# GpSimd's weight splits in the input and up projections of a two-layer encoder trunk, done by accumulating transfers from the fourth pair on

## Chip, cores and metric

One Trainium2 chip, one core. The metric is the time of one execution of the program on the device in microseconds (us): the median of three runs of the kernel before, 2488.0 us (2484.28 to 2490.77). In the text PE is TensorE, ACT is ScalarE, DVE is VectorE, POOL is GpSimd and SP is SyncE.

## What is computed

The program runs two layers on a sequence of 1024 positions with 1024 features, all in float32. Per layer:

```
h = rmsnorm(x, norm1_w)
q, k, v, g, z, xbc, dt, lru_gate, lru_x = split(h @ w_in)       # input projection
y = concat(retention(q, k, v, g), ssd(z, xbc, dt), rglru(lru_gate, lru_x))
x = x + y @ w_out
h = rmsnorm(x, norm2_w)
u, v = split(causal_conv3(h @ w_up))                            # up projection, 2 x 2816 columns
x = x + (gelu(u) * v) @ w_down
```

A last RMSNorm follows the second layer. The change touches the weights of the two products `h @ w_in` and `h @ w_up`.

## The kernel before

**Precision.** Every matrix operand is kept as two tiles of the fp32r type: the high part `hi`, a rounded copy, and the low part `lo = raw - hi`. A product is three passes over the pair: hi with hi, hi with the low part of the activations, and the low part of the weights with hi. PE therefore reads the low part of a weight tile in the third pass, behind two passes that need the high part alone.

**Splitting a weight.** `part_split` (L232) makes the two parts of a 128 x 512 piece: ACT writes the high part (L233), then DVE or POOL subtracts (L234). `lo_engine` hands the subtraction out in turn: in the input and up projections every third one goes to DVE, the other two to POOL (`share[0] = 3`). The two parts are the halves of one tile named `ws`; there are eight such tiles.

**Pairs.** The columns of both projections are worked off in pairs of 128-column tiles (class `Pair`), 12 pairs for `w_in` and 22 for `w_up` in each layer. A pair is computed with a Strassen-like scheme: seven products of twelve 128 x 512 matmuls each. Two raw tiles `wr` of 128 x 1024 (three buffers) are loaded per pair; the first holds blocks a11 and a12, the second a21 and a22. `start` splits a11 and a12 and makes two products. `prep` then works on the raw tiles in place: DVE subtracts a21 from a11 and a second tile `s2` is made from a22 and that; POOL adds a22 to a21 and subtracts `s2` from a12 (all L706); each of the five results is split. `end` makes five products, and DVE and ACT fetch all of them from PSUM. What comes out goes through a causal convolution (`conv`: ACT L311, then DVE L314, one instruction per tap), an activation, and to DRAM.

**Order.** `products` walks the pairs. The first three of each projection have another form (`lead`, `start(True)`), so that PE has work while the norm of the second half of the sequence is being computed; from `j = 3` on a pair is `start` and `end`. The order of the instructions on each engine is decided when the program is built, by a scheduler that goes by its own estimates of durations; each engine then runs its list in order and waits on semaphores.

**Stages** of the profiled execution, by its times: the fourth and later pairs of the input projection run from 113 to 343 us and from 1332 to 1548 us, those of the up projection from 627 to 995 us and from 1836 to 2205 us. Between them lie the mixers with the output projection, and the down projection.

Of the kernel before, what the change touches and what calls it, by code (L numbers as in the profile page):

```python
# [8 lines left out]
F32 = mybir.dt.float32  # L9
F32R = mybir.dt.float32r  # L10
I32 = mybir.dt.int32
AF = mybir.ActivationFunctionType
ALU = mybir.AluOpType
# [37 lines left out]
def hybrid_trunk(  # L51
# [13 lines left out]
    act, dve, pool, pe, sp = nc.scalar, nc.vector, nc.gpsimd, nc.tensor, nc.sync  # L65
# [131 lines left out]
    def lo_engine():  # L197
        flip[0] += 1
        return dve if flip[0] % share[0] == 0 else pool
# [20 lines left out]
    def wsplit(src, n=KD * P):  # L220

        raw = wr.tile([P, 2 * HT], F32, tag="wr", name=nm("wr"))
        last_dma[0] = sp.dma_start(raw[:, :n], src)
        out_ = []
        m = n // 2
        for o in (0, m):
            w = w_tile()
            part_split(w, raw[:, o : o + m], m)
            out_.append(w)
        return out_  # L230

    def part_split(w, raw, m, eng=None):  # L232
        act.activation(w[:, 0, :m], raw, AF.Copy)  # L233
        (eng or lo_engine()).tensor_tensor(w[:, 1, :m], raw, w[:, 0, :m].bitcast(F32), op=ALU.subtract)  # L234

    def wk(w):
        return lambda k, a: w[k // 4][:, a, P * (k % 4) : P * (k % 4) + P]
# [534 lines left out]
    def part_of(src):  # L772
        w = w_tile()
        part_split(w, src, HT)
        return w
# [117 lines left out]
    def products(pairs, rest, later, lead, ahead, raw=False):  # L893

        n = lead + ahead
        for j, p in enumerate(pairs[:n]):
            if j < lead:
                p.lead(raw)
            else:
                p.start(True, raw)  # L900
            if j < n - 1:
                rest(j)
        rest(2)
        for j, p in enumerate(pairs):
            if j >= n:
                p.start()
            elif raw:
                p.scaled()
            if j == 1:
                rest(3)  # L910
            if j < lead:
                p.follow()
            else:
                p.end()
            for f in later.get(j, ()):
                f()

    def ffn_pair(l, j, B):
        u = {}

        def take(m, h, x, then=None):
            cw = fcw[:, l, 2 * j + m, :]
            t = t_tile("fc")
            conv(t, x, lambda i: cw[:, i : i + 1], cw[:, 3:4], 3, not h, then)
            if m == 0:
                u[h] = t
                act.activation(t, t, AF.Gelu_apprx_tanh)  # L927
                return
            dve.tensor_mul(t, u[h], t)
            sp.dma_start(gscr[l][j][:, h, :], t)  # L930

        return Pair((w_up[l, 2 * j], w_up[l, 2 * j + 1]), B, take)
# [30 lines left out]
    def ffn_down(l, after):  # L963
# [95 lines left out]
        def last(lo=0, hi=HT, hook=None):  # L1059

            e = slice(lo, hi)
            for i in range(NP):
                w = W[i]
                t = w_tile()
                part_split(t[:, :, e], G[i][1][:, e], hi - lo, pool)
                for oc in range(4):
                    for k, (x, y) in enumerate(PASSES):
                        pe.matmul(X[oc][:, e], w[x][:, P * oc : P * oc + P], t[:, y, e], start=False, stop=i == NP - 1 and k == 2, skip_group_check=True)
                if hook:
                    hook(i)  # L1070
            for o in range(4):
                dve.tensor_add(u[o][:, e], u[o][:, e], X[o][:, e])
# [338 lines left out]
```

## Time and profile before

| | |
|---|---|
| three runs, median | 2488.0 us |
| lowest, highest | 2484.28, 2490.77 us |
| the profiled execution, own time | 2486.72 us |
| its span, first to last instruction | 2484.9 us |
| PE busy | 2236.0 us, 90% of the span |
| DVE busy | 2120.7 us, 85% |
| POOL busy | 1258.0 us, 51% |
| ACT busy | 1125.4 us, 45% |
| busy share of the 16 DMA engines (queue 1, issued by SP) | 36.3% |
| mean granted clock of PE | 0.956 |

The shares are means over stages with different limits, so the prediction reads each stage by itself: busy time by stretch, groups of instructions by line in a stretch, and who waited for whom. A duration given for one instruction is that of a row. The granted clock is a fraction of PE's full speed.

### The profile page before, as it was taken

Reading aid. Unit: us, or ns where it says so; the run is one execution under the profiler, and the core shown is the slowest. Engines: PE = TensorE matmul, PEld = TensorE weight load, DVE = VectorE, ACT = ScalarE, POOL = GpSimd, SP = SyncE. Lnnn points to the kernel's source line nnn. Section 1 sums busy time; section 2 is a strip of 40 time slices with the busy share of each in tenths; the row PEclk is TensorE's granted clock in tenths of the full one; section 3 lists DMA queues with packets and bytes.
Section 4 is the critical chain, followed back from the end, with each engine's and each line's share of the span. In section 5 each row is a group of like instructions: output and inputs, shape, how many; then the busy total and the mean of one; then the engine's idle time right before and its main releaser. Section 6 shows DMA issues by size and latency. Waiting matters only on the chain. (4 is left out here: it accounts for less than half of the span.)

```text
span 2484.9 us, 31513 instructions
## 1 busy us (share of the span) xinstructions
PE 2236.0 (90%) x10646; PEld 1774.6 (71%) x10646; DVE 2120.7 (85%) x3242; ACT 1125.4 (45%) x2110; POOL 1258.0 (51%) x846
## 2 busy tenths in 40 slices
PE   6788888997999999889988889789889999988997
PEld 4566667775888887667765768677668888866776
DVE  7998879668999999987789977785799999999787
ACT  4335437454344444434443463664534444443343
POOL 4545543346555455554655444334475555547443
PEclk8989989999999999999989989899999999999999
DMA  4321267551222222844333214846322222255521
GB/s 172 98 82 65 81 222 231 157 195 43 94 85 77 85 77 85 272 155 127 102 111 102 85 51 142 284 127 197 128 72 77 77 86 84 77 191 179 170 75 69
DMA packets 138706, 303.76 MB, mean 122 GB/s; under 512 B 15280, under 2 KB 27696, under 8 KB 138544
## 3 DMA queue, kind: packets, MB, share of 16 engines
q1 hardware_dynamic: 135760, 297.55, 36.3%
q10 hardware_dynamic: 2784, 4.20, 0.5%
q8 instruction: 84, 1.38, 0.2%
q14 instruction: 78, 0.64, 0.1%
HBM read 228.22 MB, written 69.27 MB: 120 GB/s over the span
## 5 line engine op out<-in xcount | busy, mean ns | idle before, releaser
L296 PE MATMUL up<-bh,ws 128*128 128x512 f32 x3840 | 1228.0, 399 | 46.0 <-ACT bh L202 17.3
L296 PEld LDWEIGHTS up<-bh,ws 128*128 128x128 f32 x3840 | 735.1, 192 | 224.4 <-ACT bh L202 25.3
L234 POOL TENSOR_TENSOR ws<-wr,ws 128x512 fp32r<-128x512 f32 x386 | 573.1, 1496 | 461.6 <-ACT ws L233 453.0
L296 PE MATMUL up<-bl,ws 128*128 128x512 f32 x1920 | 763.5, 399 | 40.7 <-DVE bl L203 20.5
L233 ACT ACTIVATE ws<-wr 128x512 fp32r<-128x512 f32 x568 | 340.0, 621 | 307.0 <-issue 73.3
L296 PEld LDWEIGHTS up<-bl,ws 128*128 128x128 f32 x1920 | 368.8, 192 | 137.3 <-DVE bl L203 29.6
L991 PE MATMUL dy<-ws,ws 128*128 128x512 f32 x792 | 219.3, 417 | 38.2 <-DVE ws L234 16.0
L314 DVE SCALAR_TENSOR_TENSOR fc<-u,smalls,fc 128x512 f32<-128x512 f32 (+2 forms) x176 | 215.1, 1225 | 25.7 <-ACT fc L311 24.4
L706 POOL TENSOR_TENSOR wr<-wr 128x512 f32<-128x512 f32 x64 | 114.1, 1783 | 216.7 <-DVE wr L706 192.6
L991 PEld LDWEIGHTS dy<-ws,ws 128*128 128x128 f32 x792 | 149.7, 196 | 97.4 <-DVE ws L234 36.1
L314 DVE SCALAR_TENSOR_TENSOR fc<-c,smalls,fc 128x512 f32<-128x512 f32 (+2 forms) x176 | 211.7, 1203 | 7.4 <-ACT fc L311 7.2
L991 PE MATMUL dx<-ws,ws 128*128 128x512 f32 x792 | 196.3, 398 | 1.5 <-DVE u L888 1.4
L234 DVE TENSOR_TENSOR ws<-wr,ws 128x512 fp32r<-128x512 f32 x182 | 160.0, 879 | 28.1 <-ACT ws L233 25.0
L991 PEld LDWEIGHTS dx<-ws,ws 128*128 128x128 f32 x792 | 152.7, 193 | 35.0 <-DVE u L888 1.8
L311 ACT ACTIVATE fc<-c,smalls 128x512 f32<-128x512 f32 x88 | 71.2, 810 | 214.3 <-DVE c L835 211.9
L296 PE MATMUL op<-yh,ws 128*128 128x512 f32 x512 | 162.4, 395 | 2.9 <-ACT yh L210 2.9
L706 POOL TENSOR_TENSOR wr<-wr,s 128x512 f32<-128x512 f32 x64 | 92.9, 1452 | 118.6 <-DVE u L316 97.3
L927 ACT ACTIVATE fc<-fc 128x512 f32<-128x512 f32 x88 | 55.7, 633 | 169.2 <-DVE fc L314 169.0
L234 DVE TENSOR_TENSOR ws<-g,ws 128x512 fp32r<-128x512 f32 (+1 forms) x94 | 113.9, 1238 | 20.8 <-ACT ws L233 20.6
L296 PEld LDWEIGHTS op<-yh,ws 128*128 128x128 f32 x512 | 95.5, 188 | 24.1 <-ACT yh L210 4.6
L234 POOL TENSOR_TENSOR ws<-g,ws 128x512 fp32r<-128x512 f32 (+1 forms) x71 | 103.4, 1466 | 3.8 <-ACT ws L233 3.0
L296 PE MATMUL op<-yl,ws 128*128 128x512 f32 x256 | 100.9, 397 | 1.3 <-DVE yl L215 0.8
(316 smaller groups left out, 3413.0 us busy)
## 6 DMA issues: line engine op xcount, KB each, us to landing
wr<-in_w_up_dram SPq DMA_DIRECT2D x96, 512.0 KB, 3.8
wr<-in_w_dn_dram SPq DMA_DIRECT2D x66, 512.0 KB, 3.6
wr<-in_w_ct_dram SPq DMA_DIRECT2D x56, 512.0 KB, 3.7
wr<-in_w_o_dram SPq DMA_DIRECT2D x32, 512.0 KB, 4.9
g0scr<-fc SPq DMA_DIRECT2D x44, 256.0 KB, 2.1
g<-g0scr SPq DMA_DIRECT2D x44, 256.0 KB, 5.6
g1scr<-fc SPq DMA_DIRECT2D x44, 256.0 KB, 2.1
g<-g1scr SPq DMA_DIRECT2D x44, 256.0 KB, 5.5
```

The costliest lines, as they stand in the source:

```text
L233: act.activation(w[:, 0, :m], raw, AF.Copy)
L234: (eng or lo_engine()).tensor_tensor(w[:, 1, :m], raw, w[:, 0, :m].bitcast(F32), op=ALU.subtract)
L296: pe.matmul(dst, W(k, a), A(k, b), start=first and i == 0, stop=last and i == n - 1)
L311: act.activation(dst, body(x), AF.Identity, bias=bias, scale=taps(n))
L314: dve.scalar_tensor_tensor(dst[:, o:HT], x[:, HALO - j + o : HALO - j + HT], taps(n - j), dst[:, o:HT], op0=ALU.mult, op1=ALU.add)
L706: eng.tensor_tensor(o, a, b, op=op)
L927: act.activation(t, t, AF.Gelu_apprx_tanh)
L991: pe.matmul(d[oc], w[:, a, P * oc : P * oc + P], t[:, b], start=not more and i == 0 and k == 0, stop=i == NP - 1 and k == 2, skip_group_ch ...
```

## The change

From the fourth pair of each projection on, a split that falls to POOL is no longer a subtraction on POOL. ACT writes the high part as before, then a second ACT instruction writes the negated high part into the low half, and a transfer issued from POOL's queue adds the raw weights onto it, from SBUF to SBUF. Splits that fall to DVE, and all splits of the first three pairs, of the output and the down projection, stay as they are.

```diff
+    by_dma = [False]
+
     def part_split(w, raw, m, eng=None):
         act.activation(w[:, 0, :m], raw, AF.Copy)
-        (eng or lo_engine()).tensor_tensor(w[:, 1, :m], raw, w[:, 0, :m].bitcast(F32), op=ALU.subtract)
+        eng = eng or lo_engine()
+        if eng is pool and by_dma[0]:
+
+            act.activation(w[:, 1, :m], w[:, 0, :m].bitcast(F32), AF.Copy, scale=-1.0)
+            pool.dma_start(w[:, 1, :m].bitcast(F32), raw, accum_op=ALU.add)
+            return
+        eng.tensor_tensor(w[:, 1, :m], raw, w[:, 0, :m].bitcast(F32), op=ALU.subtract)
...
         for j, p in enumerate(pairs):
+            by_dma[0] = j >= n
             if j >= n:
                 p.start()
...
             for f in later.get(j, ()):
                 f()
+        by_dma[0] = False
```

In the built program POOL's list has 851 rows before and after. 260 of its subtractions have become transfers (`DMA`, L240), and ACT's list has 261 more `ACTIVATE` rows. Lines behind L234 move by 8 to 10. The scheduler has also placed other instructions anew; two places matter for what follows.

POOL, one pair of the up projection in the first layer. `wr1260` is the pair's first raw tile (a11 and a12), `wr1268` its second; `ws1261` and `ws1262` are the splits of a11 and a12, the later `ws` those of the five combinations; `s21269` is `s2`. In brackets stands whose semaphores a row waits for (DMAHW: a transfer issued by SP or ACT, DMASW: one issued by POOL). Before:

```order
261 L234 TENSOR_TENSOR ws1261_6702<-wr1260_6700,ws1261_6702 128x512 [waits DMAHW1_49,Activation_49]
262 L706 TENSOR_TENSOR wr1268_6744<-wr1268_6744 128x512 [waits DMAHW4_49,DVE_49]
263 L234 TENSOR_TENSOR ws1262_6705<-wr1260_6700,ws1262_6705 128x512 [waits PE_49,Activation_49]
264 L706 TENSOR_TENSOR wr1260_6700<-wr1260_6700,s21269_6747 128x512 [waits DVE_49,Pool_49]
265 L234 TENSOR_TENSOR ws1271_6752<-wr1260_6700,ws1271_6752 128x512 [waits Activation_49]
266 L234 TENSOR_TENSOR ws1272_6756<-wr1268_6744,ws1272_6756 128x512 [waits Activation_49]
267 L234 TENSOR_TENSOR ws1274_6763<-wr1268_6744,ws1274_6763 128x512 [waits Activation_49]
```

The same rows in the changed program:

```order
261 L240 DMA ws1261_6776<-wr1260_6774 128x512 [waits DMASW5_49,DMASW2_49,DMAHW1_49,PE_49,Activation_49]
262 L240 DMA ws1262_6780<-wr1260_6774 128x512 [waits PE_49,Activation_49]
263 L714 TENSOR_TENSOR wr1268_6820<-wr1268_6820 128x512 [waits DMAHW4_49,DMASW1_49,DVE_49]
264 L714 TENSOR_TENSOR wr1260_6774<-wr1260_6774,s21269_6823 128x512 [waits DMASW3_49,DVE_49]
265 L240 DMA ws1271_6828<-wr1260_6774 128x512 [waits DMASW7_49,PE_49,Activation_49]
266 L240 DMA ws1272_6833<-wr1268_6820 128x512 [waits PE_49,Activation_49,Pool_49]
267 L240 DMA ws1274_6841<-wr1268_6820 128x512 [waits PE_49,Activation_49]
```

Five of the seven rows have become transfers, and the subtraction from a12 (row 264) now waits for the landing of the transfer in row 262, which reads a12.

DVE, at the same pair: its two subtractions on the raw tiles, and around them the convolution of the pair before (`fc`), the products of the up projection with `gelu` (L929) and the fetching of products from PSUM (`u`, `c` from `up`). Before:

```order
1070 L888 TENSOR_TENSOR u31227_6479<-u31227_6479,up1232_6516 128x512 [waits PE_49]
1071 L316 COPY c221228_6480<-u31227_6479 128x2 [waits DVE_49]
1072 L706 TENSOR_TENSOR wr1260_6700<-wr1260_6700,wr1268_6744 128x512 [waits DMAHW4_49,DMAHW1_49,Pool_49]
1073 L706 TENSOR_TENSOR s21269_6747<-wr1268_6744,wr1260_6700 128x512 [waits DVE_49]
1074 L314 SCALAR_TENSOR_TENSOR fc1233_6530<-u31227_6479,smalls_123,fc1233_6530 128x511 [waits Activation_49]
1075 L314 SCALAR_TENSOR_TENSOR fc1234_6537<-c221228_6480,smalls_123,fc1234_6537 128x512 [waits DMAHW2_49,Activation_49]
1076 L314 SCALAR_TENSOR_TENSOR fc1233_6530<-u31227_6479,smalls_123,fc1233_6530 128x510 [waits DVE_49]
```

In the changed program:

```order
1070 L896 TENSOR_TENSOR u31227_6549<-u31227_6549,up1232_6586 128x512 [waits PE_49]
1071 L324 COPY c221228_6550<-u31227_6549 128x2 [waits DVE_49]
1072 L322 SCALAR_TENSOR_TENSOR fc1233_6600<-u31227_6549,smalls_123,fc1233_6600 128x511 [waits Activation_49]
1073 L322 SCALAR_TENSOR_TENSOR fc1234_6607<-c221228_6550,smalls_123,fc1234_6607 128x512 [waits DMAHW2_49,DVE_49,Activation_49]
1074 L322 SCALAR_TENSOR_TENSOR fc1233_6600<-u31227_6549,smalls_123,fc1233_6600 128x510 [waits DVE_49]
1075 L322 SCALAR_TENSOR_TENSOR fc1234_6607<-c221228_6550,smalls_123,fc1234_6607 128x512 [waits DVE_49]
1076 L939 TENSOR_TENSOR fc1233_6600<-fc1217_6490,fc1233_6600 128x512 [waits DVE_49]
1077 L939 TENSOR_TENSOR fc1234_6607<-fc1231_6581,fc1234_6607 128x512 [waits DVE_49]
1078 L843 TENSOR_TENSOR c111241_6650<-u1240_6636,up1239_6623 128x512 [waits DMAHW3_49,PE_49,Activation_49]
1079 L714 TENSOR_TENSOR wr1260_6774<-wr1260_6774,wr1268_6820 128x512 [waits DMAHW1_49,DMAHW4_49,DMASW5_49,DMASW2_49]
```

The subtraction on `wr1260` has moved behind four taps, two products and the fetch of `up1239`, and it waits for the landing of the transfer that splits a11.

## Rows read from the trace of the kernel before

**Rows 1.** The page's first part: busy time, share of the span, instructions.
```profile
PE 2236.0 (90%) x10646; PEld 1774.6 (71%) x10646; DVE 2120.7 (85%) x3242; ACT 1125.4 (45%) x2110; POOL 1258.0 (51%) x846
```

**Rows 2.** Busy time by stretch: us, PE, PEld, DVE, ACT, POOL, granted clock, DMA share, GB/s.
```profile
113.00:343.00 230.00, 193.98 (x798) 150.49 (x796) 195.21 (x281) 100.79 (x165) 118.40 (x77) 0.93 0.27 89
...
627.00:995.00 368.00, 364.99 (x1600) 298.97 (x1599) 346.14 (x438) 157.90 (x260) 189.99 (x127) 1.00 0.24 84
...
1332.00:1548.00 216.00, 195.28 (x804) 151.77 (x803) 180.16 (x263) 101.10 (x166) 100.07 (x68) 0.93 0.26 87
...
1836.00:2205.00 369.00, 366.17 (x1603) 299.79 (x1602) 346.95 (x439) 158.17 (x260) 190.72 (x128) 1.00 0.24 84
```

**Rows 3.** The same of line L234 alone (the subtraction): us, DVE, POOL, clock, DMA.
```profile
113.00:343.00 230.00, 22.76 (x22) 63.48 (x43) 0.93 0.27 89
627.00:995.00 368.00, 39.21 (x45) 130.41 (x89) 1.00 0.24 84
```

**Rows 4.** In order of time, up projection: start us, us, engine, line, operation, out<-in.
```profile
740.50 0.33 SPq L779 DMA_DIRECT2D wr<-in_w_up_dram  x1
...
745.96 1.74 POOL L234 TENSOR_TENSOR ws<-wr,ws 128x512 fp32r<-128x512 f32 x1
...
746.48 1.77 DVE L314 SCALAR_TENSOR_TENSOR fc<-u,smalls,fc 128x510 f32<-128x510 f32 x1
...
748.18 0.74 DVE L314 SCALAR_TENSOR_TENSOR fc<-c,smalls,fc 128x512 f32<-128x512 f32 x1
```

**Rows 5.** Groups by line, DVE, 627 to 995 us: count | busy us, mean ns.
```profile
L314 DVE SCALAR_TENSOR_TENSOR fc<-c,smalls,fc 128x512 f32<-128x512 f32 (+1 forms) x74 | 93.3, 1261 | 3.5 <-ACT fc L311 3.5
L314 DVE SCALAR_TENSOR_TENSOR fc<-u,smalls,fc 128x510 f32<-128x510 f32 (+2 forms) x75 | 92.3, 1233 | 11.3 <-ACT fc L311 10.6
```

**Rows 6.** Groups by line, DVE, 113 to 343 us.
```profile
L314 DVE SCALAR_TENSOR_TENSOR xb<-c,smalls,xb 128x512 f32<-128x512 f32 (+3 forms) x23 | 21.5, 935 | 0.0
...
L314 DVE SCALAR_TENSOR_TENSOR xc<-u,smalls,xc 128x511 f32<-128x511 f32 (+2 forms) x6 | 6.4, 1075 | 0.0
```

**Rows 7.** Who PE waited for, 113 to 343 us: us in total, times, longest.
```profile
PE lgp L349 <- DVE xc L314: 15.5, 3, 8.5
PE cum L502 <- DVE da L499: 6.6, 1, 6.6
PE dtt L414 <- DVE dtc L409: 5.0, 1, 5.0
```

**Rows 8.** The same, 1332 to 1548 us.
```profile
PE lgp L349 <- DVE xc L314: 7.9, 2, 5.5
...
PE dtt L414 <- DVE dtc L411: 4.1, 1, 4.1
```

**Rows 9.** The same, 343 to 400 us.
```profile
PE up L296 <- DVE u L872: 6.1, 1, 6.1
```

**Rows 10.** The same, 995 to 1060 us.
```profile
PE dy L991 <- DVE u L877: 4.3, 1, 4.3
```

**Rows 11.** The same, 2205 to 2265 us.
```profile
PE dy L991 <- DVE u L877: 4.6, 1, 4.6
```

**Rows 12.** The same, whole span.
```profile
PE up L296 <- POOL ws L234: 2.0, 2, 1.6
```

**Rows 13.** DMA issues, 627 to 995 us: count, KB each, median us from issue to landing.
```profile
wr<-in_w_up_dram SPq DMA_DIRECT2D x36, 512.0 KB, 4.0
g0scr<-fc SPq DMA_DIRECT2D x38, 256.0 KB, 2.1
...
a<-in_w_dn_dram SPq DMA_DIRECT2D x2, 256.0 KB, 3.4
```

**Rows 14.** The page's part on DMA issues, whole span.
```profile
g<-g0scr SPq DMA_DIRECT2D x44, 256.0 KB, 5.6
```

**Rows 15.** The page's costliest groups, whole span.
```profile
L234 POOL TENSOR_TENSOR ws<-wr,ws 128x512 fp32r<-128x512 f32 x386 | 573.1, 1496 | 461.6 <-ACT ws L233 453.0
...
L233 ACT ACTIVATE ws<-wr 128x512 fp32r<-128x512 f32 x568 | 340.0, 621 | 307.0 <-issue 73.3
```

## The prediction

> **What bounds the kernel now.** I read the busy shares first [rows 1]. PE has 90%, DVE 85%, POOL 51%, ACT 45%: two engines lie close together, and which of them decides must be read by stretch. The table by stretch [rows 2] gives the four stretches in which splits change. In the two of the up projection PE is busy for 364.99 of 368 us and 366.17 of 369 at a granted clock of 1.00. There PE is the bound, and at most 3.0 + 2.8 = 5.8 us can be won. In the two of the input projection it is busy for 193.98 of 230 us and 195.28 of 216, at a clock of 0.93, so 36.0 + 20.7 = 56.7 us of PE time lie open. The list of waits says for whom: most of what it names is DVE, 15.5 + 6.6 + 5.0 = 27.1 us in the first input stretch [rows 7] and 7.9 + 4.1 = 12.0 in the second [rows 8]. Right behind the stretches PE waits again for DVE to empty PSUM: 6.1, 4.3 and 4.6 us [rows 9 to 11]. For a split by POOL it waits 2.0 us in the whole run [rows 12]. So in the input stretches, and where the stretches end, DVE's lateness costs PE time. POOL's splits are early enough.
>
> Then the rows in order of time [rows 4]. A tap on DVE takes 1.77 us while a split runs on POOL (745.96 to 747.70 us), and 0.74 us when none does. POOL's work thus makes DVE's instructions longer, and that is the way by which this change can win.
>
> **The change, part by part.**
>
> *260 subtractions leave POOL.* One costs 1.50 us [rows 15]. POOL waits for others half the time, so its own freed time is worth nothing; what counts is DVE's. In the up projection the taps take 74 x (1.261 - 0.74) + 75 x (1.233 - 0.74) = 38.6 + 37.0 = 75.6 us more than undisturbed [rows 4, 5]. The splits are 130.4 of POOL's 190.0 us there [rows 2, 3], 69%, so some 52 us of DVE's 346 go in 19 pairs, 2.7 us a pair. In an input stretch the bounds lie further apart. From above: 75.6/190.0 = 0.40 us of DVE for one us of POOL, times 63.5 us of splits [rows 3], 25 us. From below, two groups of taps alone: 23 x (0.935 - 0.74) + 6 x (1.075 - 0.74) = 6.5 us [rows 6], of which the splits' share (63.5 of 118.4) is 3.5 us. I take 15 us, nearer to the upper end since rows 6 are two groups out of many, and 14 for the second stretch: 29 us.
>
> How much of that does PE see? None if other waits take over, at most all 29. DVE is busy for 85 and 83% of these stretches and PE for 84 and 90%, so either bounds a part; I take three fifths, **-17 us**. In the up projection I take half of the 5.8, **-3 us**. At the ends of the stretches DVE will be less far behind; of 6.1 + 4.3 + 4.6 = 15.0 us I take two thirds, **-10 us**.
>
> *261 ACT instructions are added,* 0.62 us each [rows 15], 160 us over the four stretches, in which ACT is busy for 43 to 47% of the time [rows 2]. They lie beside PE's work and cost nothing as long as ACT is not late. Without that cover each would cost its 0.62 us, and one of them stands in the chain of every split.
>
> *260 transfers of 256 KB are added.* No row shows a transfer issued by POOL. Its issue I bound by SP's 0.33 us [rows 4] and by the 1.50 us of the instruction it replaces [rows 15], and take 1.0, between them. Its landing I bound by a plain store of this size, 2.1 us [rows 13], and by twice the landing of a load in the busiest stretch, 2 x 5.6 = 11.2 us [rows 14], because the accumulation reads two operands. I take 3.4, the load of this size into SBUF in the same stretch [rows 13], since the DMA engines are busy only 24 to 27% there [rows 2]. A split then ends later by 0.62 + 1.0 + 3.4 - 1.50 = 3.5 us; even with the lowest ends it ends later, by 1.6 us, so nothing is won by the transfer itself. For the price of a DMA from GpSimd, the Trainium skill, page "DMA: Bandwidth & Descriptors", section "Anatomy of one DMA — SWDGE (gpsimd) path", gives a fit of 2.0 us plus the bytes over 436 GB/s, by which 256 KB would take an estimated 2.6 us in all and the delay would be 1.7 us; no run here shows it.
>
> Where does the delay show? PE now waits twice for a split by POOL [rows 12]; both waits grow by 3.5: **+7 us**. All other splits have something in hand, and they start earlier where DVE, whose subtractions on the raw tiles stand ahead of them, is less late.
>
> *New waits.* The order of the changed program lets DVE's subtraction from a11 wait for the landing of a11's own split, and POOL's subtraction from a12 for the landing of a12's. Behind the first stand DVE's taps and all its fetches from PSUM, for which PE waits; behind the second POOL's further issues. In the up projection eight DVE instructions stand between the fetch of the last product and that subtraction, about 8 x 0.74 = 5.9 us. Meanwhile the split of a11 needs the fetch (0.74), three ACT instructions (3 x 0.62) and then issue and landing: 2.6 us plus 4.4. That is 1.1 us late, and DVE, with (346 - 52)/19 = 15.5 us of work in the 19.4 us of a pair, has 3.9 us to spare. So issue and landing together may take 3.3 + 3.9 = **7.2 us** before PE notices. The ring of raw tiles says much the same: load 4.0 [rows 13], two subtractions on DVE 1.5, one on POOL 1.5, seven ACT instructions 4.3, issue and landing 4.4 make 15.7 of 19.4 us, which bears 8.1 us of issue and landing. I therefore cost these waits at nothing, covered by PE's 19.4 us a pair.
>
> **Sum.** -17 - 3 - 10 + 7 = -23 us on the profiled execution's 2486.7 gives 2463.7. The median of the runs shown is 1.3 us above that execution, so I forecast **2465 us**.
>
> **The rivals.**
>
> *The relief does not reach the end.* If POOL holds DVE up while it makes a transfer, for the 1.0 us that I take instead of 1.50, only a third of the relief is left: -6 - 1 - 3 + 7 = -3, some 2485 us. Or the other waits of the input stretches (on ACT, on the clock) take over. For it: PE is as busy as DVE there. Against it: 39 us of waits name DVE. Chance 0.18; range 2478 to 2497.
>
> *Landings come late.* Place: DVE's subtraction from a11, in the two pairs of three whose a11 falls to POOL, 25 of the 38 pairs of the up projection. Price: 25 us for every us of issue and landing beyond 7.2. At 9 us that is +45; with two thirds of the gain kept, -16, 2487 + 29 = some 2515 us. At the upper ends, 1.5 + 11.2 = 12.7 us, it would be over 130 us. For it: DVE is busy for 94% of these stretches [rows 2], and a split on POOL takes up to 1.74 us where DVE works beside it [rows 4]; a transfer's issue from POOL could be held up likewise, and by more than one DVE instruction. Against it: the transfers of this stretch land in 2.1 to 4.0 us [rows 13]. The Trainium skill speaks for it on its page "SBUF — State Buffer", section "SBUF: two separate sides": a DMA issued from GpSimd starves while VectorE runs an instruction in a two-port performance mode, because GpSimd cannot write the descriptors then. In this kernel's stretches the DVE groups of rows 5 and 6 are two-input instructions, of which the same page, section "Who interferes with whom", says only by inference that they leave descriptor writing alone; the stretched 1.74 us agree with the shared port and do not settle that. Chance 0.22.
>
> *My forecast* has 0.60, with a range of its own from 2438 to 2479: below, three quarters of all that is open (39.1 + 5.8 + 15.0 = 59.9, so -45 and no late splits, 2443 with the median's 1.3, and a little for the granted clock of 0.93); above, two thirds of the gain lost.
>
> **How the numbers follow.** A measurement of this kernel can tell 0.3%, 7.5 us, from no change, so faster means under 2480.5 and slower over 2495.5. The forecast's 0.60 is faster nearly whole; of the second case's 0.18 I put 0.02 to faster, 0.14 to same and 0.02 to slower; the third's 0.22 is slower nearly whole, with 0.01 in same. That makes 0.61, 0.15 and 0.24. The range reaches from 2438 to 2515: below it some 0.05 is left out, above it half of the third case, 0.11.
>
> **What would show it.** Right: in the up projection the taps' mean falls from 1.23 to 1.26 us to about 0.9; DVE's busy time there falls from 346 to some 295 us, with PE still at 99%; PE's waits for `xc` and `da` shrink; the two input stretches are some 17 us shorter together; the new transfers land in 3 to 5 us. The second case would show taps as long as before, or PE's waits moved to ACT. The third would show landings over 7 us, DVE's idle time ended by them at the subtraction on `wr`, and up projection stretches longer than 368 us. I am wrong altogether if PE's waits for splits come to more than some 20 us although landings are short.

## The result, and the profile after

The changed kernel takes **2448.1 us** (median of four runs, 2444.9 to 2449.1) against 2489.4 (2484.3 to 2493.2): ratio **0.9834**, 95% interval 0.9822 to 0.9846. That is 41 us less; 23 were forecast.

Of the page after, the busy time (before: [rows 1]) and the two largest DMA queues, of which `q0` is new and holds GpSimd's transfers:

```profile
PE 2220.8 (91%) x10646; PEld 1771.0 (72%) x10646; DVE 1967.6 (80%) x3242; ACT 1278.5 (52%) x2370; POOL 1096.3 (45%) x846
...
q1 hardware_dynamic: 135760, 297.55, 37.5%
q0 software_dynamic: 37440, 68.17, 16.6%
```

[Rows 2] are cut at fixed times. To compare kernels I cut at PE's products instead: a stretch begins with the first product of the fourth pair and ends with the last product of that projection, so that its length (second column) is the time for the same work. Four lines each: input and up projection of the first layer, then of the second. The columns are those of [rows 2]. Busy time by stretch, before:

```profile
139.00:360.00 221.00, 191.14 (x784) 151.66 (x782) 186.18 (x262) 97.95 (x161) 117.50 (x75) 0.93 0.32 104
636.00:1004.00 368.00, 364.96 (x1598) 298.64 (x1596) 345.39 (x437) 161.56 (x266) 192.84 (x127) 1.00 0.25 87
1355.00:1563.00 208.00, 189.96 (x785) 149.96 (x783) 171.63 (x247) 98.19 (x162) 97.11 (x66) 0.94 0.32 106
1845.00:2213.00 368.00, 365.17 (x1599) 298.88 (x1597) 345.20 (x436) 161.19 (x265) 191.87 (x127) 1.00 0.25 87
```

and after:

```profile
138.00:349.00 211.00, 187.01 (x788) 148.29 (x787) 162.74 (x263) 118.46 (x207) 87.75 (x73) 0.96 0.66 167
629.00:991.00 362.00, 362.00 (x1599) 299.97 (x1598) 296.98 (x446) 215.34 (x355) 140.63 (x129) 1.00 0.67 158
1336.00:1549.00 213.00, 188.49 (x786) 149.29 (x785) 151.19 (x238) 121.53 (x211) 71.16 (x64) 0.94 0.65 165
1824.00:2186.00 362.00, 362.00 (x1598) 299.65 (x1597) 298.19 (x447) 216.96 (x356) 141.03 (x129) 1.00 0.67 160
```

DVE loses 20 to 48 us in every stretch, as it should. The up projections now run without a gap (PE 362.00 of 362.00). The first input projection is 10 us shorter, the second 5 us longer. Read to a tenth from the same products' rows (the first three pairs of each projection and the first steps of a layer are left out; the differences add up to 37.2 of the 37.9 us between the two spans):

| stretch, us | before | after | difference |
|---|---|---|---|
| input projections, two layers | 220.9, 207.7 | 210.8, 212.8 | -10.1, +5.1 |
| from there to the first product of the up projection | 190.8, 196.8 | 193.8, 189.6 | +3.0, -7.2 |
| up projections | 367.7, 367.7 | 361.8, 361.9 | -5.9, -5.8 |
| down projection; second one and the end | 216.6, 264.1 | 210.8, 253.6 | -5.8, -10.5 |

Behind the up projections PE does its own work faster. Busy time by stretch of the first down projection, before and after:

```profile
1004.00:1220.00 216.00, 197.49 (x791) 151.23 (x792) 186.54 (x206) 91.07 (x160) 119.42 (x79) 0.94 0.51 165
```
```profile
991.00:1202.00 211.00, 194.04 (x795) 147.80 (x794) 178.53 (x194) 88.95 (x157) 117.10 (x76) 0.98 0.49 158
```

The same products keep PE busy for 194.0 us instead of 197.5, at a granted clock of 0.98 instead of 0.94: PE stands at the lower of its two levels (1.2 and 2.4 GHz) for 6.8 us of this stretch, before for 23.9.

DVE's taps, 629 to 991 us (before, in [rows 5]: 1261 and 1233 ns):

```profile
L322 DVE SCALAR_TENSOR_TENSOR fc<-c,smalls,fc 128x512 f32<-128x512 f32 (+1 forms) x76 | 76.5, 1006 | 0.7 <-ACT fc L319 0.7
L322 DVE SCALAR_TENSOR_TENSOR fc<-u,smalls,fc 128x512 f32<-128x512 f32 (+1 forms) x76 | 56.8, 748 | 15.6 <-ACT fc L319 14.0
```

The two traces show instruction by instruction where this comes from. In the first up projection before, the 40 taps of 150 that ran beside no two-input operation of GpSimd took 0.74 to 0.75 us each; the 110 that ran beside one took 0.74 to 1.82, 1.42 on average. After the change 105 of 152 have none beside them and take 0.74 to 0.75 us, also the 41 of these that run beside the issue of a transfer; the other 47, beside the additions and subtractions that GpSimd still does, take 1.17 on average. VectorE's fetches from PSUM, which read one of their inputs there, take 0.68 us on average either way.

The transfers: busy time on POOL with the mean in ns, then median us to landing, counted from the start of the issue:

```profile
L240 POOL DMA_DIRECT2D ws<-wr x222 | 198.4, 910 | 252.4 <-ACT ws L239 151.4 <-issue 37.4 <-PE up L304 24.6
```
```profile
ws<-wr POOLq DMA_DIRECT2D x222, 256.0 KB, 4.2
ws<-s POOLq DMA_DIRECT2D x38, 256.0 KB, 3.3
```

Who PE waited for, whole span (us, times, longest). The wait for `xc` was 15.5 + 7.9 us in two stretches [rows 7, 8]. The first line, before and after; 10.5 and 10.9 us of it after are one wait each at the last pair of the two input projections:

```profile
PE up L296 <- ACT ws L233: 11.1, 3, 7.9
```

```profile
PE up L304 <- ACT ws L235: 33.4, 5, 10.9
...
PE lgp L357 <- DVE xc L322: 18.6, 8, 4.9
...
PE up L304 <- DMA ws<-wr: 6.8, 3, 4.0
```

### The profile page after: what moved, and what is told of

It is laid out like the page before. It is cut to its first block, busy times and chain, and to the rows that moved or that the text cites. A ratio compares the mean times of both kernels' runs of the same rounds, so it can differ in the third digit from the quotient of the medians.

```text
span 2447.0 us, 32235 instructions
## 1 busy us (share of the span) xinstructions
PE 2220.8 (91%) x10646; PEld 1771.0 (72%) x10646; DVE 1967.6 (80%) x3242; ACT 1278.5 (52%) x2370; POOL 1096.3 (45%) x846
## 3 DMA queue, kind: packets, MB, share of 16 engines
q1 hardware_dynamic: 135760, 297.55, 37.5%
q0 software_dynamic: 37440, 68.17, 16.6%
## 5 line engine op out<-in xcount | busy, mean ns | idle before, releaser
L304 PE MATMUL up<-bh,ws 128*128 128x512 f32 x3840 | 1222.4, 399 | 59.8 <-ACT ws L235 33.4
L304 PE MATMUL up<-bl,ws 128*128 128x512 f32 x1920 | 763.8, 399 | 38.4 <-DVE bl L203 19.4
L242 POOL TENSOR_TENSOR ws<-wr,ws 128x512 fp32r<-128x512 f32 x164 | 241.8, 1483 | 268.1 <-ACT ws L235 252.2
L240 POOL DMA_DIRECT2D ws<-wr x222 | 198.4, 910 | 252.4 <-ACT ws L239 151.4
L714 POOL TENSOR_TENSOR wr<-wr 128x512 f32<-128x512 f32 x64 | 104.7, 1635 | 347.3 <-DVE wr L714 214.8
L1001 PEld LDWEIGHTS dx<-ws,ws 128*128 128x128 f32 x792 | 149.3, 189 | 37.7 <-DVE u L896 4.7
L322 DVE SCALAR_TENSOR_TENSOR fc<-c,smalls,fc 128x512 f32<-128x512 f32 (+2 forms) x176 | 175.1, 995 | 1.6 <-ACT fc L319 1.4
L242 DVE TENSOR_TENSOR ws<-wr,ws 128x512 fp32r<-128x512 f32 x182 | 142.0, 781 | 37.3 <-ACT ws L235 33.9
L322 DVE SCALAR_TENSOR_TENSOR fc<-u,smalls,fc 128x512 f32<-128x512 f32 (+2 forms) x176 | 140.4, 800 | 35.4 <-ACT fc L319 32.6
L239 ACT ACTIVATE ws<-ws 128x512 fp32r<-128x512 f32 x260 | 159.5, 625 | 4.6
L714 POOL TENSOR_TENSOR wr<-wr,s 128x512 f32<-128x512 f32 x64 | 103.4, 1615 | 58.3 <-DVE s L714 50.1
L714 DVE TENSOR_TENSOR wr<-wr,wr 128x512 f32<-128x512 f32 x64 | 45.1, 704 | 87.4 <-DMA wr<-in_w_up_dram 41.1
```

The source lines that it names most:

```text
L239: act.activation(w[:, 1, :m], w[:, 0, :m].bitcast(F32), AF.Copy, scale=-1.0)
L240: pool.dma_start(w[:, 1, :m].bitcast(F32), raw, accum_op=ALU.add)
L242: eng.tensor_tensor(w[:, 1, :m], raw, w[:, 0, :m].bitcast(F32), op=ALU.subtract)
L304: pe.matmul(dst, W(k, a), A(k, b), start=first and i == 0, stop=last and i == n - 1)
L322: dve.scalar_tensor_tensor(dst[:, o:HT], x[:, HALO - j + o : HALO - j + HT], taps(n - j), dst[:, o:HT], op0=ALU.mult, op1=ALU.add)
L714: eng.tensor_tensor(o, a, b, op=op)
```

## The experiments

The theory after this look: GpSimd's subtractions lengthen VectorE's two-input instructions, and the gain is their absence; the landings are covered, save at the ends of the input projections. Rivals: the gain is another order of the instructions, or splits that are done earlier; the cost lies in the transfers' bytes. Ratios are to the kernel before on the same chip.

**Which projection gains.** Transfers in one kind of projection only:

```diff
-            by_dma[0] = j >= n
+            by_dma[0] = j >= n and len(pairs) == NF      # e_ffn; e_in has !=
```

> Transfers only in the two up projections; the input projections split on GpSimd as before. Theory (each stage's gain is its own): the two up projections and what follows them gain what they gained with the whole change (5.9 and 5.8 us in the up projections, 5.8 and 10.5 us in the down projections), the input projections nothing: some 2461 us, 2455 to 2470. Rival (most of the gain is the input projections', as the prediction had it): 2475 us or more.

> Transfers only in the two input projections; the up projections split on GpSimd as before. Theory (each stage's gain is its own, by the steps between the same products of the two traces: 10.1 us gained and 5.1 lost in the input projections, 2.4 and 11.3 gained in the mixers, 5.4 and 4.1 lost in the output projections): 2475 to 2483 us. Rival (the input projections carry most of the gain, 17 us or more): 2472 us or less. If both this and the kernel with transfers only in the up projections come near 2489, the gain needs both.

Measured: **0.9882** (0.9868 to 0.9897; 2465.1 us) and **0.9955** (0.9938 to 0.9972; 2483.2 us). The gains of 1.18% and 0.45% add up to 1.63%, the whole change's 1.66%. With transfers in the up projections alone, these run at 361.9 and 362.4 us and the two stretches behind them are 3.3 and 9.9 us shorter. So seven tenths of the gain come from the up projections, where the prediction put -3 us and some 6 of the -10 behind the stretches; transfers in the input projections give a net 11 us.

**No transfers at all.** The addition of the raw tile is left out with them, so that the results differ:

```diff
-            pool.dma_start(w[:, 1, :m].bitcast(F32), raw, accum_op=ALU.add)
```

> Leaves the transfers out, and with them the addition of the raw tile: the low part is the negated high part alone, so that the results differ. Everything else of the change stays, ScalarE's extra operation with it. What is missing is the landing of 3.3 to 9.5 us, GpSimd's 0.9 us of issue and the transfers' share of the queues. Theory (the landing is covered by the 7.2 us of VectorE's first subtraction nearly everywhere, and what is left of its cost lies at the last pair of each input projection): 2425 to 2440 us, the gain of 10 to 20 us at the ends of the two input projections, the two up projections unchanged at 362 us. Rival (the landings cost little even there, those waits being the arithmetic's own): 2443 to 2449 us. Rival (landings hold the whole pipeline back): under 2420 us with shorter steps in the up projection too.

Measured: **0.9651** (0.9632 to 0.9670; 2407.6 us): beyond the theory's 2425, and as fast as the second rival had it, but without its shorter up projections. Busy time by stretch:

```profile
138.00:331.00 193.00, 184.81 (x782) 147.79 (x780) 158.19 (x254) 117.45 (x197) 57.41 (x36) 0.97 0.35 114
614.00:975.00 361.00, 361.00 (x1595) 299.01 (x1594) 300.09 (x447) 220.91 (x357) 67.82 (x42) 1.00 0.31 99
1319.00:1509.00 190.00, 183.33 (x785) 147.20 (x783) 150.07 (x231) 120.47 (x200) 41.13 (x28) 0.98 0.37 122
1784.00:2146.00 362.00, 362.00 (x1599) 299.85 (x1598) 300.16 (x448) 221.47 (x358) 68.22 (x42) 1.00 0.30 99
```

The removal of the subtractions is worth 87 us, and the transfers give 46 of it back (the difference of the ratios, 0.0183, times 2495). Nearly all of what they cost lies in the input projections, 18 and 23 us; in the up projections they cost nothing. PE itself has a part in the gain: from the kernel before to this one its busy time in the input projections falls from 191.14 to 184.81 and from 189.96 to 183.33 us, at a granted clock of 0.97 and 0.98 instead of 0.93 and 0.94.

**Is the gain VectorE's relief?** The first attempt ran the old subtraction ahead of each transfer:

```diff
+            pool.tensor_tensor(w[:, 1, :m], raw, w[:, 0, :m].bitcast(F32), op=ALU.subtract)
             act.activation(w[:, 1, :m], w[:, 0, :m].bitcast(F32), AF.Copy, scale=-1.0)
```

> Every split that the change gives to a transfer first runs the old GpSimd subtraction as well, into the place that the negated high part then overwrites; the transfers, their queue, ScalarE's extra operation and the emission order stay. Theory (GpSimd's subtractions stretch VectorE's two-input operations, and the gain is their absence): VectorE's taps on PSUM in the first up projection, 1006 and 748 ns after the change, go back to 1.2 us, VectorE's busy time there from 297 to 340 us or more, the up projection no longer runs at the full rate of its products (365 us and more instead of 362), and the time is 2480 us or more, the split being some 1.5 us later as well. Rival (the gain comes from another order of the instructions or from how the transfers are queued): 2445 to 2460 us with both stages at 362 us, whatever the taps take.

Measured: 1.0983 (1.0966 to 1.1000). It tells little of the theory: the up projections took 464 and 462 us, but the taps did not come back to 1.2 us, and PE's largest wait was for the landings themselves:

```profile
PE up L305 <- DMA ws<-s: 137.2, 32, 7.1
```

Each split now went to ScalarE, GpSimd, ScalarE and GpSimd again, each time behind other work. The better test leaves the transfers and the addition out and gives GpSimd its operation back where no product waits for its result, seven times a pair:

```diff
-            pool.dma_start(w[:, 1, :m].bitcast(F32), raw, accum_op=ALU.add)
+            for _ in range(in_prep[0]):        # 1, and 2 for the last two of prep's five splits
+                pool.tensor_tensor(raw, raw, raw, op=ALU.add)        # e_pool
+                pool.tensor_tensor(raw, raw, w[:, 0, :m].bitcast(F32), op=ALU.subtract)    # e_pool2 instead
```

> No transfers, low parts are the negated high parts (the addition is left out), but GpSimd gets its old work back where nothing of the products waits for it: after each of the five splits of sums and differences it adds the raw tile to itself in place, twice for two of them, seven two-input operations for the seven subtractions of a pair that are gone (the doubled values then feed one later difference). Theory (GpSimd's two-input operations stretch VectorE's, and this is what made the up projections slower than the products): VectorE's taps in the up projections go back from 0.75 to 1.0 us to 1.15 to 1.26, its busy time there from 300 to 335 us or more, the up projections take 365 us or more instead of 361.8, and the ratio is 0.98 to 1.00 instead of 0.965. Rival (the gain is that splits are done earlier, by an engine that is not busy): taps may go up, but the up projections stay at 362 us and the ratio at 0.965 to 0.972.

> As the kernel with GpSimd's additions in place (no transfers, low parts are the negated high parts, the addition of the raw tile is left out), but the operation is the old one in all but its destination: raw tile minus high part, from two tiles, written over the raw tile; seven per pair, and no product waits for them (one later difference then works on other values). The additions in place took 1.15 to 1.23 us, the old subtractions 1.51, and VectorE's busy time in the up projections came to 322 us, between 300 without and 345 in the kernel before; they still ran at the full rate of 361.8. Theory (VectorE's stretched operations bound the up projections in the kernel before): the taps go to 1.2 us or more, VectorE's busy time there to 335 to 345 us, the up projections to 363 us or more, ratio 0.980 to 0.995. Rival (what bound them was that products waited for GpSimd's results): VectorE's busy time as high, but the up projections at 361.8 to 362.4, ratio below 0.982, the cost at the input projections alone.

Measured: **0.9794** (0.9775 to 0.9813) and **0.9945** (0.9928 to 0.9961; 2478.7 us). Of the second, busy time by stretch, and GpSimd's operation in the first up projection:

```profile
138.00:365.00 227.00, 190.22 (x784) 151.31 (x782) 189.76 (x261) 119.67 (x202) 117.59 (x76) 0.91 0.31 99
647.00:1009.00 362.00, 362.00 (x1598) 299.85 (x1598) 329.88 (x439) 216.82 (x355) 196.62 (x128) 1.00 0.28 91
1361.00:1570.00 209.00, 188.93 (x784) 149.34 (x782) 171.45 (x237) 119.73 (x200) 97.42 (x67) 0.95 0.33 106
1852.00:2214.00 362.00, 362.00 (x1598) 299.75 (x1598) 329.95 (x440) 217.09 (x356) 196.94 (x128) 1.00 0.28 91
```
```profile
L242 POOL TENSOR_TENSOR wr<-wr,ws 128x512 f32<-128x512 f32 x75 | 108.7, 1456 | 43.3 <-ACT ws L236 40.5
```

GpSimd's busy time is that of the kernel before again (117.6, 196.6, 97.4, 196.9). No product reads what it writes, yet 73 of the 87 us are lost again (0.0294 of 2492). The input projections go from 193 and 190 us to 227 and 209, and DVE's busy time in them to what it was before. The first of the two runs, whose in-place additions took 1.14 to 1.23 us, lies between, with 179 and 166 us of DVE and stretches of 216 and 199; of its two expectations neither came whole. So in the input projections the stretch follows VectorE's busy time. One other thing came back with the operation: it writes the raw tile, and SyncE waits for GpSimd to release such tiles (49.6 and 51.7 us in the two input projections). That is a small part of the 34 and 19 us: the run that spares two pairs, below, has 51.2 and 52.3 us of such waits, for landings, in input projections of 204 and 195 us.

The theory fails for the up projections as I had stated it. The taps come to 1073 and 1104 ns, not 1.2 us, DVE to 330 us, not 335 to 345, and PE stays at the products' own rate. What held the up projections at 368 us is seen in the trace of the kernel before. All waits of products in that stretch, 636 to 1004 us, name VectorE; none of them, and none of the weight loads', names a result of GpSimd:

```profile
PE up L296 <- DVE u L872: 1.7, 3, 0.8
PE up L296 <- DVE ws L234: 1.1, 3, 0.4
```

Of the steps from one product to the next 21 are longer than 0.24 us, by 5.5 us in all. They lie at two places of a pair: 3.6 us at the first product of `end`, behind VectorE's fetch from PSUM, and 1.9 us at the third pass of the second product of `start`, behind a split of VectorE's own. So VectorE's lateness held them. With 330 us of work, in the order of this run, VectorE is not late.

**What do the transfers cost by?** They still run, but into scratch tiles off the core (the addition is left out of the low part, which does not wait for them); then the same with an eighth of the bytes:

```diff
-            pool.dma_start(w[:, 1, :m].bitcast(F32), raw, accum_op=ALU.add)
+            pool.dma_start(far[turn[0] % 8][:, :m], raw, accum_op=ALU.add)        # e_traffic
+            pool.dma_start(far[turn[0] % 8], raw[:, :64], accum_op=ALU.add)       # e_hold instead
+            turn[0] += 1
```

> The low part is the negated high part alone, as in the kernel without transfers (the addition is left out, so that results differ), but each transfer still runs with the same source, size and accumulation, into scratch tiles in memory off the core that nothing waits for; eight more transfers fill these at the start. So the traffic and GpSimd's issue are back, the wait of the products for the landing is not. Theory (what the transfers cost is their landing, waited for at the last pairs of the input projections): the ratio to the kernel before stays near that without transfers, 0.965 to 0.970, both input projections from the fourth pair on at 190 to 195 us. Rival (what they cost is their load on the DMA engines, which delays the input projections' own loads, the rotation tables' and the convolution weights' among them): 0.978 to 0.984 as with the whole change, the input projections at 205 to 213 us. Between the two the share of each is read.

> As the kernel whose transfers go to scratch tiles that nothing waits for (the addition is left out, low parts are the negated high parts), but each transfer takes 64 of the 512 columns, an eighth of the bytes. It still holds the loaded tile until it has landed, and GpSimd still issues it. Theory (what transfers cost beyond the kernel without them is that they hold the loaded tiles longer in the ring of three, and the orders that follow from it): near the full-size scratch transfers less their start-up, 0.977 to 0.983. Rival (it is their bytes on the DMA engines): near the kernel without transfers, 0.965 to 0.970.

Measured: **0.9826** (0.9797 to 0.9855) and **0.9709** (0.9690 to 0.9728). The eight first fills made the start of the former some 10 us longer, so that its own ratio is about 0.979. Input projections: 210.0 and 193.6 us with all bytes (the first as the rival had it, the second as the theory), 204.0 and 189.3 with an eighth. Both expectations of e_hold miss: between them, with a rise of 11 us in the first layer and none in the second. By the differences of the ratios, holding the tiles and issuing costs some 14 us, the bytes 19 more, waiting for the landings the last 12. The next run warns against reading these as prices: each of these programs has its own order.

**Later and with twice the bytes**, by way of a scratch tile:

```diff
-            pool.dma_start(w[:, 1, :m].bitcast(F32), raw, accum_op=ALU.add)
+            pool.dma_start(far[turn[0] % 16][:, :m], raw)
+            pool.dma_start(w[:, 1, :m].bitcast(F32), far[turn[0] % 16][:, :m], accum_op=ALU.add)
+            turn[0] += 1
```

> Each raw tile first goes by a GpSimd transfer into memory off the core and is added from there, so that a split is done some 4 to 5 us later and GpSimd issues twice (0.9 us more); the traffic of these splits doubles. The prediction's threshold says that issue and landing together are covered up to 7.2 us, the time from VectorE's first subtraction on the tile, and that each microsecond beyond costs about as much per pair. Here they come to 9 to 11 us. Theory (threshold): the up projections go over 362 us, to 390 us and more, ratio 1.01 or more. Rival (the products' order leaves far more room than 7.2 us): the up projections stay within 365 us and the ratio below 0.995, the loss at the input projections alone.

Measured: **0.9854** (0.9830 to 0.9878). The interval overlaps that of the change: twice the bytes and a much later landing cost next to nothing net. In the first up projection, median us to landing:

```profile
ws<-far POOLq DMA_DIRECT2D x87, 256.0 KB, 5.8
far<-wr POOLq DMA_DIRECT2D x72, 256.0 KB, 3.6
```

One behind the other that is at least 9.4 us. The up projections take 367.7 and 373.2 us, between what the theory and the rival of the expectation gave; the ratio is the rival's. PE now waits for landings itself, whole span:

```profile
PE up L308 <- DMA ws<-far: 42.0, 8, 10.8
```

This run does not test the price that the prediction put on a late landing. Its place was VectorE's subtraction on the raw tile, and that tile is free here when the first transfer has landed, 3.6 us after its issue began; in the whole run VectorE's subtraction waits for such a landing once, 1.9 us. What the run shows is the slack of the products: low parts that land this much later cost 6 and 11 us in an up projection. The second input projection even became shorter, 197.7 us against 212.8. Bytes and landing cannot explain that; an order can.

**The order on SyncE.** Some of the projection's outputs are rotated by tables of the positions (`tb`), which SyncE loads too. Near the end of the first input projection of the change, by time: SyncE's issues, VectorE's rotation, its second subtraction for the last pair, ScalarE's high part of the result, PE's first product with it.

```profile
317.42 0.93 SPq L385 DMA_DIRECT2D tb<-in_rope_dram  x2
318.45 0.36 SPq L787 DMA_DIRECT2D wr<-in_w_ct_dram  x1
```
```profile
308.11 0.69 DVE L386 TENSOR_TENSOR u<-u,tb 128x512 f32<-128x512 f32 x1 [7.89 <-DMA qs<-u]
...
314.04 0.69 DVE L386 TENSOR_TENSOR u<-u,tb 128x512 f32<-128x512 f32 x1 [3.68 <-DMA tb<-in_rope_dram]
...
327.44 0.69 DVE L714 TENSOR_TENSOR s<-wr,wr 128x512 f32<-128x512 f32 x1
```
```profile
328.61 0.61 ACT L235 ACTIVATE ws<-s 128x512 fp32r<-128x512 f32 x1
```
```profile
329.28 0.79 PE L304 MATMUL up<-bh,ws 128*128 128x512 f32 x1 [10.50 <-ACT ws L235]
```

The load at 318.45 is the last weight tile of the projection; it lands at 323.60. SyncE issues it behind all the rotation's tables. Without transfers it goes out at 294.74, ahead of three quarters of them. Its place is one of three in the ring of loaded tiles. SyncE's longest row of waits for such a place in the first input projection, before:

```profile
SPq L779 <- POOL ws L234: 32.9, 10, 7.5
```

and after:

```profile
SPq L787 <- DMA ws<-wr: 51.3, 11, 12.5
```

These rows alone mislead: with the other waits at the same line (20.6 us for VectorE before, 4.8 for VectorE and ScalarE after) it is 53.5 us before and 56.1 after. In the second layer it grows, from 32.6 to 56.0.

Two runs spare the last pair, and the last two:

```diff
-            by_dma[0] = j >= n
+            by_dma[0] = n <= j < len(pairs) - 1      # e_notlast; e_not2 has - 2
```

> The last pair of each input and up projection splits on GpSimd as before; everything else as in the change. The trace of the change has one wait of 10.5 and one of 10.9 us of TensorE on the last pair's splits, one in each input projection. Theory (these waits are landings that nothing covers there): both input projections some 8 to 10 us shorter, 200 to 205 us, the ratio 0.976 to 0.980 or 2430 to 2440 us on a chip where the kernel before takes 2490. Rival (the last pair is late because the loads before it are, whatever splits it): the same ratio as the change, 0.982 to 0.985.

> The last two pairs of each input and up projection split on GpSimd as before; transfers from the fourth pair on up to there. In the change the last load of a convolution weight tile in each input projection stands on SyncE's queue behind the rotation's transfers and tables (issued at 318 us in the first layer; at 295 us in the kernel without transfers), because its place in the ring of three loaded tiles comes free with the transfer of the pair before the last; the kernel that spared the last pair alone had the same order. Here SyncE's order has that load before the rotation's last tables. Theory (the input projections' loss is this late load: VectorE takes the rotation first and waits 7.9 and 3.7 us there, TensorE 10.5 and 10.9): waits of TensorE on the last pair's splits fall from 10 us to 4 or less, the input projections to 195 to 204 us each, ratio 0.970 to 0.976. Rival (the loss is the load that transfers put on the DMA engines, whatever the order): input projections stay at 203 to 213 us, ratio 0.977 to 0.983.

Measured: **0.9781** (0.9753 to 0.9808; 2440.4 us) and **0.9725** (0.9710 to 0.9740; **2425.5 us**). Sparing the last pair leaves the first input projection at 212.1 us, with SyncE's order and the long wait as they were, in that stretch:

```profile
PE up L304 <- ACT ws L235: 11.0, 1, 11.0
```

so the last pair's own landings are not the cause there; the second one gains 9 us. Sparing two pairs, the ring's place comes free earlier and the last load goes out ahead of the tables, at

```profile
302.70 0.33 SPq L787 DMA_DIRECT2D wr<-in_w_ct_dram  x1
```

The input projections take 204.3 and 194.5 us, the wait of 11 us is gone, and the kernel beats both that it is compared with, the change by some 27 us (1.09% of 2494). SyncE's waits for a place are no shorter (61.3 and 60.8 us), so it is not their length that costs. The run also makes the transfers of two pairs less in each projection, so the 27 us are not the order's alone.

The other traces tell the order from the transfers. In five of the 14 kernels (the change, e_in, e_notlast, e_port, and e_prep below) the last load stands behind all table loads, in both input projections, and in each of these ten stretches PE waits 7.0 to 13.3 us for the first of the last pair's combinations. In the other nine it stands ahead of six of the eight, and there PE never waits more than 2 us for a split of that pair. Among them is e_late, with a transfer for every split of the change and twice the bytes: its last pairs take 19.2 us each, those of the change 35.3 and 37.7. In e_notlast the last pair has no transfer, and PE waits 11.0 and 7.0 us all the same. So the late place accounts for the 10.5 and 10.9 us that PE waits there in the change, half of the 41 us that transfers cost the input projections; the other half is not divided further.

**Transfers for the five combinations alone**, the two raw splits of a pair's start back on GpSimd:

```diff
-        if eng is pool and by_dma[0]:
+        if eng is pool and by_dma[0] and in_prep[0]:
```

> Only the five operands that are formed by sums and differences go by transfers; the two raw ones of a pair's start stay on GpSimd or VectorE as lo_engine gives them. VectorE's subtraction that writes into the loaded tile then waits less for transfers (29.4 us over the whole run in the trace of the change). Theory (the gain in the up projections is all had once VectorE has any slack there, and the landings cost the input projections): up projections still 362 us, ratio 0.980 to 0.985. Rival (each split moved counts in proportion): two of seven splits back is a gain smaller by two sevenths, ratio 0.987 to 0.990.

Measured: **1.0025** (1.0012 to 1.0039). Both expectations miss: it gains nothing on the kernel before, and the up projections take 379.9 and 374.8 us. Two rows grew, whole span. One is VectorE's wait for loaded tiles; after the change

```profile
DVE wr L714 <- DMA wr<-in_w_up_dram: 41.1, 16, 6.0
```

and here

```profile
DVE wr L715 <- DMA wr<-in_w_up_dram: 79.8, 33, 5.3
```

The other is PE's wait for the landings of `s2`'s splits, of which the change has none:

```profile
PE up L305 <- DMA ws<-s: 14.7, 12, 2.1
```

GpSimd's queue then holds subtractions and issues in turn, and the ring turns more slowly. Which of the two delays the loads is open.

## Why the prediction was right, and where it was not

The time lies in the range and the forecast's own case came true, with 41 us for 23. Its mechanism, VectorE's relief, held. The sum did not hold term by term: two gains were larger than forecast and one far smaller, and that the total stayed in the range is in part luck.

- *DVE's relief.* The rows came as forecast: taps 1006 and 748 ns (0.9 us forecast), DVE's busy time in an up projection 345 to 297 us (295 forecast).
- *-17 us in the input projections.* In the change the two are 5 us shorter together, -10.1 and +5.1. The term was mis-sized twice over. From the kernel before to the one without transfers DVE's busy time there falls by 28.0 and 21.6 us, and the stretches get 28.1 and 17.8 us shorter; GpSimd's work put back takes it all back. I had taken 15 and 14 us of DVE time, where the upper bound of 25 was near, and three fifths of it for the stretch, where it is nine tenths. I had no term for the granted clock: as it rises, 6.3 and 6.6 us of PE's busy time there go too. Then the transfers take 18 and 23 us back.
- *+7 us for late splits.* PE's waits for landings are 6.8 us, and that they match is chance. One of the two waits in [rows 12] belongs to the first three pairs, which the change leaves alone; all three waits for landings lie at the last pair of an input projection, behind the late load. The transfers' cost is 46 us. The step that failed is the one on new waits: I let VectorE and GpSimd wait for landings and checked the ring of raw tiles against the 19.4 us of a pair in the up projection. In the input projections SyncE's queue also carries the rotation, its tables and the stores of results; the changed program has the last load behind them, and there VectorE and PE pay. I named no cost for SyncE.
- *The sign for being wrong altogether* came true: PE's waits for splits come to 40 us (33.4 for high parts, 11.1 before, and 6.8 for landings), where I had set 20, at landings of 4.2 us. 28 us of them lie at the last pairs of the input projections, behind the late loads; the relief was large enough to cover them. The sign that the input stretches would be 17 us shorter did not come; PE's waits shrank for `da` from 6.6 to 1.3 us, for `xc` only from 23.4 to 18.6.
- *-3 us in the up projections.* The bound of 5.8 us was wrong; 11.7 were won. I read PE's busy time as its need. After the change 1599 products fill 362.00 us, 0.2264 each; before, 1598 took 368. The floor is the count times the rate of products that wait for nothing, and a busy PE hides what lies above it.
- *-10 us behind the stretches.* 16.3 us, but not by the waits that I had named: of those for `u` [rows 10, 11], 4.3 and 4.6 us, 3.0 and 0.8 are left, 5.1 less. Most of the rest is PE's busy time, 3.5 us less in each of the two stretches at a higher granted clock (0.94 to 0.98, and 0.93 to 0.95).
- *Issue and landing.* 4.2 us from the start of the issue to the landing, 0.91 of them on GpSimd (1.0 and 3.4 taken), under the 7.2 us. In the first up projection VectorE's subtraction waits 16.9 us for such landings, PE never. The fit of the Trainium skill's page "DMA: Bandwidth & Descriptors", section "Anatomy of one DMA — SWDGE (gpsimd) path", gave an estimated 2.6 us; the measurement decides.
- *The rival of late landings* did not occur in the up projections, and its price stays untested: in e_late the tile that VectorE waits for is free after 3.6 us. The *rival that the relief does not reach the end* falls with the gain, and neither engine shows itself held up by an issue: 0.85 to 1.49 us an issue in the whole run, beside a VectorE that is busy for 80% of it, and taps of 0.75 us beside issues. So the starving of GpSimd's issues, which the Trainium skill's page "SBUF — State Buffer", section "SBUF: two separate sides", ties to VectorE's two-port modes, does not show here; whether VectorE runs such a mode at all in this kernel, no row tells.

## What to carry to other kernels

Take a two-input instruction off GpSimd for what it does to VectorE, not for GpSimd's own time: in the trace, sort VectorE's instructions by what runs beside them, and then measure the worth with GpSimd's work put back where nobody waits for it. A transfer in its place holds its source until it has landed: look for the queue that loads into that source's buffer, and compare the order of its issues before and after, stage by stage, not only the length of its waits. And take TensorE's floor from the number of products and the rate of an undisturbed stretch, never from its busy share.

## What was not expected of the hardware

An accumulating transfer from SBUF to SBUF, issued by GpSimd, occupies the DMA engines longer per byte than the loads and stores of SyncE's queue: 68.17 MB take 16.6% of their time, 297.55 MB 37.5%, which is 0.244% against 0.126% per MB. Whether the accumulation, the place of source and target or the issuing queue makes it so, no run separates.

With transfers in place of some GpSimd instructions VectorE's taps can be longer beside the others: in e_hold and e_traffic DVE's busy time in the first up projection was 325 and 322 us against 297 after the change, though GpSimd was busy for no longer (133 and 131 us, 141 after the change) and did the same additions and subtractions. The traces show that these meet the taps otherwise: in e_hold 49 taps run beside one, for 1.87 us on average and up to 3.64 (47 and 1.17 us on average after the change), and the 104 others take 0.74 to 0.75 as everywhere. It cost the up projections nothing.
